# Channel-major products as 512 streamed columns over 256-column weight groups, with x scaled ahead of the products

## The chip, the cores and the metric

The kernel runs on one core of a Trainium2 chip. The metric is the device time of one execution in microseconds; lower is better. The engines are TensorE (PE, with its weight loads shown as PEld), VectorE (DVE), ScalarE (ACT), GpSimd (POOL) and SyncE (SP, which here only starts transfers). Times of stages and instructions come from one profiled execution.

## What is computed

One residual layer with three token-mixer branches over 256 tokens of width 2048, in float32. x is normalised, multiplied by one wide matrix (18464 columns), split among attention, a state-space branch and memory attention, gated, projected and summed. The part that matters here:

```python
def rms_norm(x, w):
    xf = x.astype(jnp.float32)
    y = xf * lax.rsqrt(jnp.mean(xf * xf, axis=-1, keepdims=True) + NORM_EPS)
    return (y * w.astype(jnp.float32)).astype(x.dtype)
...
    h = rms_norm(x, norm_w[layer])
    proj = h @ w_in[layer]
    (sb_q, sb_k, sb_v, sb_z, ssd_z, ssd_xbc, ssd_dt,
     mem_q, mem_z, gate_pre) = jnp.split(proj, offsets, axis=-1)
...
    mem_n = rms_norm(mem, mem_norm_w[layer])
    kv = mem_n @ w_kv
```

## The kernel before

Float32 products are made of three fast products. Every operand is split into a high part (rounded to the fast format) and a low part (what is left), and a product is high by high, high by low and low by high. `split` makes both parts: ScalarE writes the high part (line 143), VectorE subtracts it from the source (line 147, or line 149 where a scale per partition goes in). The activations are kept channel-major, channels on the partitions: `memT` for mem and `hT` for x, 16 k-tiles of 128 channels by 256 tokens, high and low parts in tiles of their own (`Cols`).

`gemm` (line 204) walks over the 16 k-tiles in chunks of two. For each chunk a 512 KB block of weights is loaded on SP's queue (`load_chunk`, `raw`, four buffers) and split into `wh` and `wl` (three buffers each), then come the matmuls, then `pump()`. There are two forms:

- rows (lines 231 to 236): the activations are the stationary operand, 512 weight columns stream past; result tokens by channels. Per k-tile 6 matmuls of 512 columns.
- columns (lines 220 to 230): 128 weight columns are stationary, 256 tokens stream past; result channel-major. Per k-tile and group of 128 weight columns three matmuls of 256 columns: `wh` with the high part, `wh` with the low part, `wl` with the high part.

Columns are used for the memory keys (1024 weight columns), for memory q, memory z, attention z, q and k (1024 each) and for the 4096 convolution channels; rows for everything else.

The order on every engine is written out by the program: nothing is reordered. `pump()` runs once per chunk. It calls what `defer(fn, n)` put n chunks ahead, and takes one step from one of two `lanes` of generators (even chunks one lane, odd chunks the other). So the work around a product stands at fixed places between its chunks; an engine takes its instructions in that order.

Normalisation before: hT is split from x times `norm_w` without the token's own factor, as soon as x is there (`x_pairs`, from the middle of the second product on). The sums of squares are made channel-major from the same x tiles: ScalarE squares 1024 elements at a time (line 296), GpSimd adds the four tiles (lines 297 to 300), TensorE sums over partitions (line 306). `scale_steps` makes 1/rms per token, as a column (`rs_x`) and spread over all partitions (`rbc_x`). That factor is applied at the end of each product that reads hT: on VectorE by a multiply with `rbc_x` (lines 247, 256, 631) for columns, as a scale per partition for rows (lines 272, 615, 770).

The start of the program is: values of the memory (two row products, 10 and 8 chunks), memory keys (two column products of 8 chunks), then memory q from hT.

Of the kernel before, what the change touches and what calls it, by code (L numbers as in the profile page):

```python
# [16 lines left out]
P = 128  # L17
# [4 lines left out]
KC = 2  # L22
EPS = 1e-6
# [3 lines left out]
XLAG = 8  # L27
# [13 lines left out]
def trunk_kernel(  # L41
    ctx: ExitStack,
    tc: tile.TileContext,
    x, x_cols, mem_cols, w_cols, w_in, b_gate, dt_bias, a_log,
# [11 lines left out]
    psA = ctx.enter_context(tc.tile_pool(name="psA", bufs=4, space=bass.MemoryType.PSUM))  # L56
# [94 lines left out]
    class Cols:  # L151


        def __init__(self, nk, n):
            self.hi = [slot([P, 8, T], F32R, n + "h") for _ in range(nk // 8)]
            self.lo = [slot([P, 8, T], F32R, n + "l") for _ in range(nk // 8)]

        def at(self, kt):
            return self.hi[kt // 8][:, kt % 8], self.lo[kt // 8][:, kt % 8]
# [44 lines left out]
    def gemm(lhs, nk, w, c0, evac, cols=False, along=None, sizes=None):  # L204


        acc = [psA.tile([P, GW], F32, tag="acc", name=nm("acc")) for _ in range(2)]
        k0 = 0
        for kc in sizes or [KC] * (nk // KC):
# [6 lines left out]
            for j in range(kc):  # L216
# [3 lines left out]
                if cols:  # L220
                    for b in range(4):
                        a = acc[b // 2][:, (b % 2) * T:(b % 2 + 1) * T]
                        bs = slice(b * P, (b + 1) * P)
                        nc.tensor.matmul(a, wh[:, j, bs], lh, start=first and b % 2 == 0,  # L224
                                         stop=False, skip_group_check=True)
                        nc.tensor.matmul(a, wh[:, j, bs], ll, start=False, stop=False,  # L226
                                         skip_group_check=True)
                        nc.tensor.matmul(a, wl[:, j, bs], lh, start=False, stop=last,  # L228
                                         skip_group_check=True)
                    continue  # L230
# [8 lines left out]
        if cols:  # L239
            acc = [a.rearrange("p (b t) -> p b t", t=T) for a in acc]  # L240
        defer(lambda: evac(acc))

    def to_cols(dst, b0, scale):

        def evac(acc):
            for pr in range(2):
                nc.vector.tensor_tensor(dst[:, b0 + 2 * pr:b0 + 2 * pr + 2], acc[pr],
                                        scale.unsqueeze(1).to_broadcast([P, 2, T]), ALU.mult)
        return evac

    def to_split_cols(dst, b0, scale):
        def evac(acc):
            parts = []
            for pr in range(2):
                u = tmp.tile([P, 2, T], F32, tag="cu", name=nm("u"), bufs=2)
                nc.vector.tensor_tensor(u, acc[pr], scale.unsqueeze(1).to_broadcast([P, 2, T]),
                                        ALU.mult)
                bs = slice(b0 + 2 * pr, b0 + 2 * pr + 2)
                parts.append((dst.hi[0][:, bs], dst.lo[0][:, bs], u, None))
            defer(lambda: split(*parts), 1)  # L260
        return evac
# [7 lines left out]
    def to_rows(dst, c0, scales):  # L269
        def evac(acc):  # L270
            for t in range(2):
                nc.scalar.activation(dst[:, t, c0:c0 + GW], acc[t], AF.Copy,
                                     scale=scales[:, t:t + 1])
        return evac
# [13 lines left out]
    def squares(raw, acc, q, first=None):  # L288

        sq = t4([P, 4, T], "sq")  # L290
        a = 0
        if first is not None:
            nc.scalar.activation(sq[:, 0], first, AF.Square)
            a = 1
        k = 4 * (q % 2)
        nc.scalar.activation(sq[:, a:4], raw[q // 2][:, k + a:k + 4], AF.Square)
        nc.gpsimd.tensor_tensor(sq[:, 0:2], sq[:, 0:2], sq[:, 2:4], ALU.add)
        if q:
            nc.gpsimd.tensor_tensor(sq[:, 0], sq[:, 0], sq[:, 1], ALU.add)
# [624 lines left out]
```

## Time and profile before

| | us |
|---|---|
| median of 3 executions | 1248.94 (1248.73 to 1250.66) |
| the profiled execution, own time | 1249.63 |
| its span | 1247.6 |
| TensorE busy | 1234.8 |
| VectorE busy | 775.9 |
| ScalarE busy | 596.3 |
| GpSimd busy | 123.2 |

The granted TensorE clock is 0.999 of full speed over the span. The stages by the first matmul of each form: row products from 5.7 us, column products from 54.5, rows from 351.4, columns (the convolution channels) from 487.3, rows from 681.5 to the end; single products of the branches run between the chunks.

A matmul's record is longer than its turn: consecutive records overlap. How long one matmul holds TensorE is read from the distance between the starts of two, not from its duration.

### The profile page before, as it was taken

What the parts mean: (1) busy time and instruction counts of PE and PEld (TensorE: products, weight loads), DVE (VectorE), ACT (ScalarE), POOL (GpSimd) and SP (SyncE); (2) the same over time, 40 slices, a digit from 0 to 9 for tenths busy, and PEclk for the clock granted to TensorE, in tenths of its full rate; (3) what the DMA queues carried; (4) which work ended last, traced back from release to release, by engine and by line L of the source; (5) the groups of instructions that cost most, each with busy time, mean ns of one, the idle gap of its engine ahead of it and who ended that gap; (6) DMA issues with size and microseconds to landing.
All of it is one profiled execution on the core that took longest, in us unless ns stands there. A gap on an engine that the chain in (4) does not pass through costs nothing.

```text
span 1247.6 us, 18787 instructions
## 1 busy us (share of the span) xinstructions
PE 1234.8 (99%) x7512; PEld 1108.9 (89%) x7512; DVE 775.9 (62%) x997; ACT 596.3 (48%) x734; POOL 123.2 (10%) x130
## 2 busy tenths in 40 slices
PE   8999999999999999999999999999999999999997
PEld 6899999999988888999999888888888888888886
DVE  7674564555544555688888876676766555555554
ACT  6643443453434545444654545555554444444443
POOL 3510000000000000010100202022211110110101
PEclk9999999999999999999999999999999999999999
DMA  8666565655566656555656656666555666567573
GB/s 295 216 209 174 164 189 174 183 158 164 153 187 197 185 174 183 169 172 169 171 174 196 217 169 220 177 223 199 190 165 182 207 198 196 189 193 245 199 238 123
DMA packets 124680, 236.57 MB, mean 190 GB/s; under 512 B 10128, under 2 KB 11568, under 8 KB 124464
## 3 DMA queue, kind: packets, MB, share of 16 engines
q1 hardware_dynamic: 118272, 224.01, 58.2%
q10 hardware_dynamic: 6320, 11.35, 2.6%
q8 instruction: 59, 0.97, 0.3%
q14 instruction: 29, 0.24, 0.1%
HBM read 233.20 MB, written 2.13 MB: 189 GB/s over the span
## 4 chain that ended last, share of the span: by engine, by line
PE 94%; DMA 2%; ACT 1%; DVE 1%; issue 1%; POOL 0%; SPq 0%; POOLq 0%; ACTq 0%; DVEq 0%
PE acc L234 17%; PE acc L236 17%; PE acc L235 17%; PE acc L224 12%; PE acc L228 12%; PE acc L226 12%; DMA raw<-in_w_mem_kv_dram 2%; PE y L709 1%; DVE wl L147 1%; PE acc L881 1%; PE acc L879 1%; PE acc L880 1%; ACT wh L143 0%; PE off L711 0%; PE dtp L401 0%
## 5 line engine op out<-in xcount | busy, mean ns | idle before, releaser
L147 DVE TENSOR_TENSOR wl<-raw,wh 128x1024 fp32r<-128x1024 f32 (+1 forms) x410 | 510.1, 1245 | 365.6 <-ACT wh L143 364.2
L143 ACT ACTIVATE wh<-raw 128x1024 fp32r<-128x1024 f32 (+1 forms) x410 | 431.9, 1054 | 523.5 <-PE acc L236 265.5
L224 PE MATMUL acc<-hTh,wh 128*128 128x256 f32 x1152 | 327.4, 284 | 0.0
L226 PE MATMUL acc<-hTl,wh 128*128 128x256 f32 x1152 | 325.9, 283 | 0.0
L228 PE MATMUL acc<-hTh,wl 128*128 128x256 f32 x1152 | 325.9, 283 | 0.0
L234 PE MATMUL acc<-wh,hTh 128*128 128x512 f32 x576 | 227.7, 395 | 0.0
L236 PE MATMUL acc<-wh,hTl 128*128 128x512 f32 x576 | 224.5, 390 | 0.0
L235 PE MATMUL acc<-wl,hTh 128*128 128x512 f32 x576 | 224.3, 389 | 0.0
L226 PEld LDWEIGHTS acc<-hTl,wh 128*128 128x128 f32 x1152 | 221.1, 192 | 0.0
L224 PEld LDWEIGHTS acc<-hTh,wh 128*128 128x128 f32 x1152 | 221.0, 192 | 0.1
L228 PEld LDWEIGHTS acc<-hTh,wl 128*128 128x128 f32 x1152 | 221.0, 192 | 0.0
L236 PEld LDWEIGHTS acc<-wh,hTl 128*128 128x128 f32 x576 | 108.1, 188 | 22.9
L235 PEld LDWEIGHTS acc<-wl,hTh 128*128 128x128 f32 x576 | 108.3, 188 | 21.7
L234 PEld LDWEIGHTS acc<-wh,hTh 128*128 128x128 f32 x576 | 108.2, 188 | 21.6
L783 POOL TENSOR_TENSOR merged<-merged,sig 128x512 f32<-128x512 f32 x16 | 27.5, 1744 | 260.2 <-DVE sig L782 222.7
L571 POOL TENSOR_TENSOR lm<-lm,sp 128x384 f32<-128x384 f32 x8 | 11.5, 1435 | 402.3 <-DVE sp L570 402.3
L234 PE MATMUL acc<-wh,oDh 128*128 128x512 f32 x128 | 49.8, 389 | 0.0
L235 PE MATMUL acc<-wl,oDh 128*128 128x512 f32 x128 | 49.8, 389 | 0.0
L236 PE MATMUL acc<-wh,oDl 128*128 128x512 f32 x128 | 49.8, 389 | 0.0
L636 DVE SCALAR_TENSOR_TENSOR cT<-cu,wcols,cT 128x255 f32<-128x255 f32 (+2 forms) x96 | 46.4, 483 | 3.4
L234 PE MATMUL acc<-wh,mTh 128*128 128x512 f32 x96 | 37.4, 390 | 0.0
L236 PE MATMUL acc<-wh,mTl 128*128 128x512 f32 x96 | 37.4, 389 | 0.0
(256 smaller groups left out, 1463.8 us busy)
## 6 DMA issues: line engine op xcount, KB each, us to landing
raw<-in_w_in_dram SPq DMA_DIRECT2D x288, 512.0 KB, 3.8
raw<-in_w_branch_ssd_dram SPq DMA_DIRECT2D x32, 512.0 KB, 4.0
raw<-in_w_out_dram SPq DMA_DIRECT2D x32, 512.0 KB, 4.7
raw<-in_w_mem_kv_dram SPq DMA_DIRECT2D x30, 512.0 KB, 4.9
raw<-in_w_branch_mem_dram SPq DMA_DIRECT2D x16, 512.0 KB, 4.4
raw<-in_w_branch_sb_dram SPq DMA_DIRECT2D x16, 512.0 KB, 4.0
dec<-acT ACTq DMA_DIRECT2D x16, 256.0 KB, 5.7
sig<-in_b_gate_dram ACTq DMA_DIRECT2D x12, 256.0 KB, 4.0
```

The source lines that it names most:

```text
L143: nc.scalar.activation(hi, src, AF.Copy, **({} if scale is None else {"scale": scale}))
L147: nc.vector.tensor_tensor(lo, src, h32, ALU.subtract)
L224: nc.tensor.matmul(a, wh[:, j, bs], lh, start=first and b % 2 == 0, stop=False, skip_group_check=True)
L226: nc.tensor.matmul(a, wh[:, j, bs], ll, start=False, stop=False, skip_group_check=True)
L228: nc.tensor.matmul(a, wl[:, j, bs], lh, start=False, stop=last, skip_group_check=True)
L234: nc.tensor.matmul(a, lh[:, tt], wh[:, j], start=first, stop=False)
L235: nc.tensor.matmul(a, lh[:, tt], wl[:, j], start=False, stop=False)
L236: nc.tensor.matmul(a, ll[:, tt], wh[:, j], start=False, stop=last)
L636: nc.vector.scalar_tensor_tensor(a[:, s:T], u[:, 0:T - s], convw[:, 3 - s, i:i + 1], a[:, s:T], ALU.mult, ALU.add)
L709: nc.tensor.matmul(y[:, q, xc], dec[e // 2][:, e % 2, q], xs[:, q, xc], start=True, stop=True)
L783: nc.gpsimd.tensor_tensor(merged[t][:, cs], merged[t][:, cs], sig[:, t], ALU.add)
L879: nc.tensor.matmul(acc, lh[:, tt], wh, start=(kt == 0), stop=False)
```

## The change

1. `gemm_cols` takes the place of the column form of `gemm`. It makes 256 weight columns at a time, in chunks of four k-tiles (again 512 KB, now 128 partitions by four rows of 256 columns, 1 KB each). High and low parts of the activations now lie side by side in one tile (`Cols.both`), so one matmul streams 512 columns, high and low, past one `wh` group; `wl` streams the 256 columns of the high part and is added to the second half of the accumulator.
2. The accumulator has two halves, which `fold` adds at the end: ScalarE copies one half out of PSUM, VectorE adds the other. The end is deferred by two chunks (`LATE_C`), in `gemm` by three as before.
3. Sums of squares come from rows: x and mem are loaded again, token-major, in four pieces of 512 KB each, on ScalarE's queue (`load_rows`), and ScalarE squares 512 elements with a running sum (`squares`, two per piece). GpSimd's adds and TensorE's sums over partitions are gone.
4. x is multiplied by `rbc_x` on VectorE before the split (`scale_pair`, line 392), so hT holds the normalised x, and no product's end multiplies by `rbc_x` or `rs_x` any more. x's channel-major load moves from the second product to the key products; its eight `scale_pair` calls stand behind chunk 5 of the keys to chunk 1 of memory q.

The core of the diff:

```diff
+    def gemm_cols(lhs, nk, w, c0, evac, ready=None):
+        acc = psA.tile([P, 2, 2, T], F32, tag="acc", name=nm("acc"), bufs=2)
+        for k0 in range(0, nk, KCC):
...
+            raw = load_chunk(w, c0, 2 * P, k0, KCC)
...
+            for kt in range(k0, k0 + KCC):
+                first, last = kt == 0, kt == nk - 1
+                for b in range(2):
+                    nc.tensor.matmul(acc[:, b], wh[:, kt - k0, b * P:(b + 1) * P],
+                                     lhs.both(kt), start=first, stop=False,
+                                     skip_group_check=True)
+                for b in range(2):
+                    nc.tensor.matmul(acc[:, b, 1], wl[:, kt - k0, b * P:(b + 1) * P],
+                                     lhs.at(kt)[0], start=False, stop=last,
+                                     skip_group_check=True)
+            pump()
+        defer(lambda: evac(acc), LATE_C)
+    def fold(dst, acc):
+        nc.scalar.activation(dst, acc[:, :, 1], AF.Copy)
+        nc.vector.tensor_tensor(dst, acc[:, :, 0], dst, ALU.add)
...
-        nc.scalar.activation(sq[:, a:4], raw[q // 2][:, k + a:k + 4], AF.Square)
-        nc.gpsimd.tensor_tensor(sq[:, 0:2], sq[:, 0:2], sq[:, 2:4], ALU.add)
...
+    def squares(r, ss, q):
+        for t in range(2):
+            nc.scalar.activation(r[t], r[t], AF.Square, accum_out=ss[:, t, q:q + 1])
...
+    def row_squares(src, ss, q):
+        r = load_rows(src, q)
+        defer(lambda: squares(r, ss, q), 3)
...
     def along1(k0):
-        if k0 % 4 == 0:
-            xload(k0, k0 + 4)
...
+        if k0 == 0:
+            row_squares(mem, ss_m, 3)
+        elif k0 < 10:
+            row_squares(x, ss_x, k0 // 2 - 1)
+        elif k0 == 10:
+            defer(lambda: scale_x(scale_steps(rs_x, rbc_x, ss_x)), 3)
+            for k in range(0, NKT, 4):
+                defer(lambda k=k: xload(k, k + 4), 1 + k // 2)
...
+    def scale_pair(k):
+        part = xraw[k // 8][:, k % 8:k % 8 + 2]
+        nc.vector.tensor_tensor(part, part, rbc_x.unsqueeze(1).to_broadcast([P, 2, T]),
+                                ALU.mult)
+        split_cols(xraw, hT, normw, k)
+        x_ready.append(k)
...
     def conv_evac(i0):
         def evac(acc):
...
+            u = tmp.tile([P, 2, T], F32, tag="cu", name=nm("cu"), bufs=2)
+            fold(u, acc)
```

How it moves instructions, at three places. First TensorE where the first key product begins, before. `acc_535` and `acc_536` are accumulators, `memTh` and `memTl` the high and low parts of mem, `wh` and `wl` those of the weights; the last figures are partitions by streamed columns.

```order
L236 MATMUL acc_58_354<-wh_87_506,memTl_5_119 128x512
L224 MATMUL acc_91_535<-memTh_2_116,wh_94_539 128x256
L226 MATMUL acc_91_535<-memTl_4_118,wh_94_539 128x256
L228 MATMUL acc_91_535<-memTh_2_116,wl_95_540 128x256
L224 MATMUL acc_91_535<-memTh_2_116,wh_94_539 128x256
```

One k-tile and 256 weight columns were six matmuls of 256 columns. The same place after the change; `memT` holds both parts, and x2 means twice in a row, once for each group of 128 weight columns.

```order
L259 MATMUL acc_58_347<-wh_103_518,memT_5_119 128x512
L332 MATMUL rbc_107_539<-dg_98_489,ones_81 128x256
L223 MATMUL acc_109_541<-memT_2_116,wh_111_544 128x512 x2
L227 MATMUL acc_109_541<-memT_2_116,wl_112_545 128x256 x2
L223 MATMUL acc_109_541<-memT_2_116,wh_111_544 128x512 x2
```

They are two matmuls of 512 columns and two of 256. Second, ScalarE in the second product (values of the memory), before: `wh` are its chunks' splits, `sq` squares, `hTh` the high part of x.

```order
L143 ACTIVATE wh_63_376<-raw_62_374 128x1024
L143 ACTIVATE wh_66_394<-raw_65_392 128x1024
L296 ACTIVATE sq_68_411<-mraw_11_125 128x1024
L143 ACTIVATE wh_72_418<-raw_71_416 128x1024
L143 ACTIVATE wh_75_436<-raw_74_434 128x1024
L143 ACTIVATE wh_79_458<-raw_78_456 128x1024
L143 ACTIVATE hTh_6_120<-xraw_12_126,wcols_80 128x256 x2
L296 ACTIVATE sq_81_478<-xraw_12_126 128x1024
```

After, in the same product: `rows` are the token-major pieces, a DMA row is the start of a load on ScalarE's own queue, and `ss_m` and `ss_x` collect the sums.

```order
L144 ACTIVATE wh_66_374<-raw_65_372 128x1024
L313 DMA rows_68_378<-in_x_dram 128x2x512
L318 ACTIVATE rows_55_331,ss_m_128<-rows_55_331 128x512 x2
L144 ACTIVATE wh_71_396<-raw_70_394 128x1024
L310 DMA rows_73_400<-in_x_dram 128x512
L310 DMA rows_74_401<-in_x_dram 128x512
L318 ACTIVATE rows_62_354,ss_m_128<-rows_62_354 128x512
L318 ACTIVATE rows_63_355,ss_m_128<-rows_63_355 128x512
```

Between two chunks' splits there now stand one or two load starts and two squares, which wait for a load started two chunks earlier. Third, VectorE in the key products, before (`kTl` is the low part of the keys, `u` a product's end, `hTl` the low part of x):

```order
L147 TENSOR_TENSOR wl_135_887<-raw_133_884,wh_134_886 128x1024
L256 TENSOR_TENSOR u_136_914<-acc_91_535,rbc_m_111 128x512
L256 TENSOR_TENSOR u_137_916<-acc_92_536,rbc_m_111 128x512
L149 SCALAR_TENSOR_TENSOR hTl_9_123<-xraw_13_127,wcols_80,hTh_7_121 128x256 x2
L147 TENSOR_TENSOR wl_141_925<-raw_139_922,wh_140_924 128x1024
L147 TENSOR_TENSOR kTl_17_131<-u_136_914,kTh_16_130 128x512
```

And after, in the second of the four key products:

```order
L148 TENSOR_TENSOR wl_158_779<-raw_156_776,wh_157_778 128x1024
L392 TENSOR_TENSOR xraw_12_126<-xraw_12_126,rbc_x_112 128x512
L150 SCALAR_TENSOR_TENSOR hT_7_121<-xraw_12_126,wcols_80,hT_7_121 128x256 x2
L236 TENSOR_TENSOR u_159_803<-acc_136_643,u_159_803 128x512
L275 TENSOR_TENSOR u_159_803<-u_159_803,rbc_m_111 128x512
L148 TENSOR_TENSOR wl_163_810<-raw_161_807,wh_162_809 128x1024
```

The multiply of x and the fold's add are new in the row of work; all eight pairs of x now stand here.

## Rows read from the trace of the kernel before

**Rows 1.** Windows: length, busy (x instructions) by engine, clock, DMA share, GB/s.

```profile
15.00:20.00 5.00, 5.00 (x24) 3.96 (x23) 4.23 (x6) 5.00 (x11) 2.90 (x2) 1.00 1.05 387
...
200.00:300.00 100.00, 100.00 (x836) 100.00 (x836) 50.98 (x56) 43.82 (x50) 0.00 (x0) 1.00 0.58 171
...
500.00:600.00 100.00, 100.00 (x823) 99.56 (x822) 79.19 (x126) 44.48 (x54) 5.55 (x3) 1.00 0.57 169
```

**Rows 2.** Timeline of PE, a column product: start, us, engine, line, operation, idle before.

```profile
200.28 0.28 PE L224 MATMUL acc<-hTh,wh 128*128 128x256 f32 x1
...
202.67 0.28 PE L228 MATMUL acc<-hTh,wl 128*128 128x256 f32 x1
```

**Rows 3.** Timeline of PE, a row product, two starts twelve matmuls apart.

```profile
33.58 0.39 PE L234 MATMUL acc<-wh,memTh 128*128 128x512 f32 x1
...
36.30 0.39 PE L234 MATMUL acc<-wh,memTh 128*128 128x512 f32 x1
```

**Rows 4.** Timeline of PE where 384 and 256 columns alternate, four matmuls.

```profile
490.16 0.34 PE L580 MATMUL scu<-sph,ra 128*128 128x384 f32 x1
490.34 0.28 PE L582 MATMUL scu<-sph,rb 128*128 128x256 f32 x1
...
490.74 0.28 PE L224 MATMUL acc<-hTh,wh 128*128 128x256 f32 x1
```

**Rows 5.** Groups by form: line, engine, operation, count | busy, mean ns | idle before, releaser.

```profile
L147 DVE TENSOR_TENSOR wl<-raw,wh 128x1024 fp32r<-128x1024 f32 x406 | 507.3, 1251 | 359.8 <-ACT wh L143 358.4
L143 ACT ACTIVATE wh<-raw 128x1024 fp32r<-128x1024 f32 x406 | 429.3, 1058 | 520.6 <-PE acc L236 265.5 <-PE acc L226 178.3 <-issue 44.5
...
L780 DVE TENSOR_TENSOR merged<-acc,sig 128x512 f32<-128x512 f32 x8 | 5.1, 681 | 0.0
L615 ACT ACTIVATE zD<-acc,rs_x 128x512 f32<-128x512 f32 x8 | 5.0, 676 | 0.0
...
L812 ACT ACTIVATE junk<-yo 128x512 f32<-128x512 f32 x6 | 3.8, 627 | 6.7 <-DVE yo L810 6.7
...
L721 ACT ACTIVATION_READ_ACCUMULATOR xs<-xn 128x1 f32 x16 | 3.0, 187 | 0.0
```

**Rows 6.** Waits of ACT, 560 to 650 us: us in total, times, longest us.

```profile
ACT wh L143 <- PE acc L226: 27.0, 17, 2.5
```

**Rows 7.** Timeline of PE, places in the first 62 us where its starts stand apart.

```profile
28.27 0.40 PE L234 MATMUL acc<-wh,memTh 128*128 128x512 f32 x1
...
29.77 0.53 PE L236 MATMUL acc<-wh,memTl 128*128 128x512 f32 x1 [0.37 <-DVE memTl L149]
...
45.83 0.50 PE L306 MATMUL ss<-ones,sq_m 128*128 128x1 f32 x4
46.19 0.49 PE L234 MATMUL acc<-wh,memTh 128*128 128x512 f32 x1
...
61.02 0.39 PE L228 MATMUL acc<-memTh,wl 128*128 128x256 f32 x1 [0.38 <-DVE wl L147]
```

**Rows 8.** Timelines of DVE, POOL and ACT: splits beside GpSimd's adds and alone, a load's start.

```profile
27.09 1.75 DVE L147 TENSOR_TENSOR wl<-raw,wh 128x1024 fp32r<-128x1024 f32 x1
...
27.84 1.59 POOL L300 TENSOR_TENSOR sq_m<-sq,sq_m 128x256 f32<-128x256 f32 x1
...
86.00 1.22 DVE L147 TENSOR_TENSOR wl<-raw,wh 128x1024 fp32r<-128x1024 f32 x1 [0.26 <-ACT wh L143]
87.14 0.87 DVE L149 SCALAR_TENSOR_TENSOR hTl<-xraw,wcols,hTh 128x256 fp32r<-128x256 f32 x2
...
0.78 0.41 ACTq L371 DMA_DIRECT2D head<-in_mem_cols_dram  x1
```

**Rows 9.** DMA issues, 20 to 45 us: queue, count, KB each, median us to landing.

```profile
xraw<-in_x_cols_dram SPq DMA_DIRECT2D x3, 512.0 KB, 8.1
```

**Rows 10.** DMA queue of the weights, whole span: packets, MB, share of 16 engines.

```profile
q1 hardware_dynamic: 118272, 224.01, 58.2%
```

**Rows 11.** DMA queue of the ACT writes, 1234 to 1247.6 us.

```profile
q10 hardware_dynamic: 576, 0.66, 13.9%
```

More of the change, by code (lines that the diff above doesn't have):

```diff
@@ L22 @@
 KC = 2
+KCC = 4
 EPS = 1e-6
@@ L154, in __init__, with at, both @@
         def __init__(self, nk, n):
[L155 to L159, printed above, removed]
+            self.hl = [slot([P, 4, 2, T], F32R, n) for _ in range(nk // 4)]
+        def at(self, kt, n=None):
+            s = self.hl[kt // 4]
+            k = kt % 4 if n is None else slice(kt % 4, kt % 4 + n)
+            return s[:, k, 0], s[:, k, 1]
+        def both(self, kt):
+            return self.hl[kt // 4][:, kt % 4]
     lanes = [deque(), deque()]
@@ L219, in gemm @@
                 first, last = kt == 0, kt == nk - 1
[L220 to L230, printed above, removed]
                 for t in range(2):
@@ L286, in split_cols, with load_rows, scale_steps @@
         split(*[(*dst.at(k), raw[k // 8][:, k % 8], w[:, k:k + 1]) for k in (k0, k0 + 1)])
[L288 to L295, printed above, removed]
-        nc.scalar.activation(sq[:, a:4], raw[q // 2][:, k + a:k + 4], AF.Square)
-        nc.gpsimd.tensor_tensor(sq[:, 0:2], sq[:, 0:2], sq[:, 2:4], ALU.add)
-        if q:
-            nc.gpsimd.tensor_tensor(sq[:, 0], sq[:, 0], sq[:, 1], ALU.add)
-        nc.gpsimd.tensor_tensor(acc, sq[:, 0], acc if q else sq[:, 1], ALU.add)
-    def scale_steps(rs, rbc, acc):
-        ps = bank([P, 2], "ss")
+    def load_rows(src, q):
+        cs = slice(q * GW, (q + 1) * GW)
+        if q % 2:
+            r = [ta([P, GW], "rows") for _ in range(2)]
+            for t in range(2):
+                nc.scalar.dma_start(r[t], src[t * P:(t + 1) * P, cs])
+            return r
+        r = t4([P, 2, GW], "rows")
+        nc.scalar.dma_start(r, src[:, cs].rearrange("(t p) n -> p t n", p=P))
+        return [r[:, t] for t in range(2)]
+    def squares(r, ss, q):
         for t in range(2):
-            nc.tensor.matmul(ps[:, t:t + 1], acc[:, t * P:(t + 1) * P], ones[:, 0:1],
-                             start=True, stop=True)
-        yield
+            nc.scalar.activation(r[t], r[t], AF.Square, accum_out=ss[:, t, q:q + 1])
+    def scale_steps(rs, rbc, ss):
         ms = small([P, 2], "ms")
-        nc.vector.tensor_scalar(ms, ps, 1.0 / D, EPS, ALU.mult, ALU.add)
+        nc.vector.tensor_reduce(ms, ss, AX.X, ALU.add)
+        nc.vector.tensor_scalar(ms, ms, 1.0 / D, EPS, ALU.mult, ALU.add)
         nc.gpsimd.tensor_tensor(rs, ms, mhalf, ALU.pow)
```

129 lines of the change are left out of this document (61 added, 68 removed).

## The prediction

> **What bounds the kernel now.** I read the windows first. From 200 to 300 us TensorE is busy all the time, in a stretch of column products, while VectorE is busy half of it and ScalarE less [rows 1]. In the convolution stage, the fullest for VectorE, TensorE is still busy all the time and VectorE 79.19 of 100 us [rows 1]. ScalarE's splits are mostly held back by TensorE: of 520.6 us idle before `wh`, 265.5 and 178.3 end with a matmul [rows 5]; in the convolution stage it waited 17 times in 90 us [rows 6]. So the other engines run ahead until the three weight buffers are full, and from about 62 us to the tail the time is the number of matmuls times the turn of each.
>
> The turn is the distance between starts. Twenty column matmuls of 256 streamed columns take 2.39 us [rows 2], 119.5 ns each; twelve row matmuls of 512 take 2.72 us [rows 3], 226.7 ns each. The clock is the full 2.4 GHz (1.00 in [rows 1]), at which 256 columns alone are 106.7 ns and 512 are 213.3. So each matmul costs its columns and about 13 ns on top, whatever its width. That a mixture keeps this law is seen where 384 and 256 columns alternate: four matmuls from 490.16 to 490.74 [rows 4], 0.58 us for 1280 columns (533 ns) and four times 12 ns.
>
> Only the start is different. Between 5 and 62 us there are places where TensorE's starts stand apart [rows 7], because VectorE is late, and transfers run at 387 GB/s with all 16 DMA engines busy [rows 1].
>
> **The change part by part.**
>
> *Fewer, wider matmuls.* Per k-tile and 256 weight columns, six turns of 119.5 ns become two of 226.7 and two of 119.5: 717.0 against 692.4 ns, 24.6 ns less. By the 13.3 ns on top of a 512-column turn it is two such amounts, 26.6. The column products have 40 groups of 256 weight columns (4 for the keys, 20 for the five blocks of 1024, 16 for the convolution), times 16 k-tiles, 640 in all: 15.7 to 17.0 us, taken as 16.3. All of it is on the path, since TensorE has no gap there. A chunk of a column product goes from 24 × 119.5 = 2.87 us to 8 × 226.7 + 8 × 119.5 = 2.77 us.
>
> A page speaks against this term: the Trainium skill, "TensorE: Matmul & The Clock Gate", section "Back-to-back issue gap", gives a gap of N/2.4 plus 2.5 ns, so a matmul saved would be worth 2.5 ns and not 13. Rows 2 and 3 differ from it, and the measured turn decides; what it would give is among the rivals.
>
> *The ends of products.* Per 512 weight columns VectorE had two multiplies out of PSUM and now has two adds, both about 0.68 us (nearest row, `merged` [rows 5]): nothing. In the convolution four multiplies of 256 elements become two adds of 512: a little less. ScalarE gets two copies of 512 elements out of PSUM, 0.68 us each (`zD` [rows 5]), 27 us over the 40 products; with `wh` at 1.06 it is then busy some 1.2 of each 2.77 us. Cover: it is up to three weight tiles ahead. What is new is a coupling: VectorE's add waits for ScalarE's copy, the copy for the product's last matmul, and behind them stand the next `wh` and `wl`. The end comes two chunks (5.5 us) after the last matmul's chunk in program order, and copy, `wh` and `wl` take 0.68 + 1.06 + 1.25 = 3.0 us. It holds with 2.5 us to spare. Bounds: 0, and 4 us (0.1 us at each of 40 ends, since a miss costs the excess alone); nearer to 0: taken 0.5.
>
> *GpSimd's adds and TensorE's partition sums go.* A `wl` split beside a GpSimd add takes 1.75 us, alone 1.22 [rows 8]. The two matmuls from 28.27 to 29.77 [rows 7] took 1.50 instead of 0.45 us, waiting for VectorE in such a stretch: 1.05 us. The sum over partitions holds TensorE from 45.83 to 46.19 [rows 7], 0.36 us, and once more for x: 0.7. The wait at 61.02 [rows 7] costs about 0.5. Together −2.3 us.
>
> *Row pieces in the first two products.* Eight loads of 512 KB (4.2 MB) join from the eighth chunk on, while x's channel-major 2.1 MB move to the keys, where there is room. Over about 25 us the demand is nine weight chunks (4.7 MB) and the rows, 8.9 MB or 356 GB/s against the 387 seen [rows 1]: near full. A 512 KB load in the crowded stretch landed after 8.1 us [rows 9]; the squares come about two chunks (5.4 us) after the start, so ScalarE can stand up to 2.7 us. Its work per chunk is `wh` 1.06, two squares of 0.63 with a read of the sum of 0.19 each [rows 5], 1.63, and one or two load starts of 0.41 [rows 8]: 3.1 to 3.5 us against TensorE's 2.72 for twelve row matmuls. Over seven chunks that is 2.7 to 5.6 us of lead used up, with the 2.7 at most 8.3. Against it stands a lead of two chunks and the squares that go earlier in the first product. Bounds 0 and 8 us. I take 1.5, near the lower end, because ScalarE is normally ahead [rows 5].
>
> *x scaled in the key products.* For each of eight pairs VectorE does the multiply (0.68), waits for ScalarE's first half (0.5), does two low parts (0.87 [rows 8]), waits about 0.5 for `wh`, then `wl` (1.22): 3.8 us where a chunk lasts 2.77. Eight pairs, five chunks with `wl` alone, and three ends of keys with a fold, a multiply and a low part (2.0) make 42.5 us in 13 chunks, which last 36.0. The excess of 6.5 us meets a lead of two to three chunks (5.5 to 8). Bounds 0 and 4 us, taken 1.5.
>
> *DMA shape.* The weights of column products come in rows of 1 KB. The whole weight queue used 58.2% of 16 engines' 1247.6 us for 118272 packets, nearly all of 2 KB [rows 10]: 98 ns each. The writes at the end, 1.15 KB a packet on average, took 13.9% of 16 × 13.6 us for 576 [rows 11]: 52.5 ns. By that a chunk's 512 packets need 512 × 52.5/16 = 1.68 us of 2.77: hidden, cost nothing. What if not is the last rival.
>
> *Sum,* on the profiled execution (1249.6 of its own, span 1247.6): 1249.6 − 16.3 − 2.3 + 0.5 + 1.5 + 1.5 = 1234.5. The median shown is 0.7 lower, so 1233.8, rounded to 1233.5.
>
> **The rivals.**
>
> - *The start is dear.* The row loads and the scaling cost their upper bounds, 8 and 4 us instead of 3 together: 1242.5. For it: the 8.1 us landing and the 356 of 387 GB/s. Against it: four `raw` buffers and ScalarE's lead.
> - *A matmul saved is worth little.* If the 13 ns came with streamed columns and not with each matmul, and only 2.5 ns went with each, the gain is 640 × 2 × 2.5 ns = 3.2 us: 1246.5. Rows 2 to 4 speak against it. It is the page's rule named above.
> - *The column stages stop following TensorE.* VectorE and ScalarE wait for each other so long that the chunk stays at 2.87 us: the gain is lost, and the start's 1.2 us are added: about 1250. For it: VectorE is at 79% in the convolution. Against it: ScalarE's waits for TensorE there [rows 6].
> - *The 1 KB rows make the weight transfers the bound: slower.* It decides from 86.6 ns a packet on (16 × 2.77 us/512). If a 1 KB packet took as long as a 2 KB one, 98 ns, a chunk would need 3.14 us, and the 160 chunks of column products 160 × (3.14 − 2.87) = 43 us more than before: 1249.6 + 43 + 1.2 − 0.7 = 1293. Rows 11 speak against it, though they are writes.
>
> **How the numbers follow.** The forecast, 1228 to 1239, has 0.72; the dear start 0.13; the small saving 0.03; the lost gain 0.05; the slow transfers 0.07. The low end of the range, 1228, is the sum with 17.0 us and the three open terms at 0 to 0.5 (1249.6 − 0.7 − 17.0 − 2.3 − 1 for what GpSimd's absence may give beyond the two places). The high end, 1242, reaches to the dear start and leaves out the last three. A measurement of this kernel tells about 0.2% from no change, 2.5 us. Faster by more: 0.72 + 0.13 = 0.85; within: 0.03 + 0.05 = 0.08; slower: 0.07.
>
> **What would show it.** After the change 16 column matmuls should take 2.77 us, with no idle time of TensorE between 100 us and the tail; a window of 100 us in the column stages should hold some 578 matmuls. `wl` in the first 60 us should take 1.2 us, not 1.75. The weight queue's share in the column stages should stay under 0.75. The places to look for new waits are ScalarE's squares between 25 and 50 us (released by a load of `rows`) and VectorE's splits between 65 and 100 us. I am wrong if the turn in the alternation is not 226.7 and 119.5, if TensorE waits for `wl` or `wh` in the column stages, or if the start loses more than 8 us.

## The result, and the profile of the changed kernel

The changed kernel takes 1236.8 us (1235.77 to 1237.86), the kernel before, run beside it, 1249.07 us (1248.73 to 1250.66). The ratio is 0.9899, with a 95% interval of 0.9882 to 0.9916: 12.3 us or 1.0% faster. Forecast were 1233.5 us, in a range of 1228 to 1242.

The profiled execution of the changed kernel took 1237.6 us, with a span of 1235.9; before, these were 1249.63 and 1247.6. The two spans differ by 11.7 us. The first matmuls of each stage show where that lies:

| from the first matmul of ... to the next stage's | before, us | after, us | change |
|---|---|---|---|
| start, row products of mem | 48.77 | 49.14 | +0.4 |
| column products up to the first row product of the middle | 296.89 | 288.77 | -8.1 |
| row products of the middle | 135.91 | 135.91 | 0 |
| convolution, column products | 194.26 | 188.51 | -5.75 |
| last row products, to the last matmul | 557.55 | 559.08 | +1.5 |
| after the last matmul | | | +0.24 |

So 13.9 us were won where column products run, and about 2 us lost elsewhere. The windows of after, the changed kernel (length, busy time and count by engine, granted clock, DMA share, GB/s), answer to [rows 1]:

```profile
100.00:200.00 100.00, 100.00 (x590) 87.71 (x589) 58.76 (x84) 46.45 (x57) 0.46 (x1) 1.00 0.65 185
200.00:300.00 100.00, 100.00 (x594) 88.08 (x594) 54.74 (x59) 49.61 (x60) 0.00 (x0) 1.00 0.59 176
500.00:600.00 100.00, 100.00 (x579) 87.65 (x579) 85.46 (x136) 52.41 (x67) 7.39 (x4) 1.00 0.59 178
```

TensorE is still busy all the time in the column stages, now with 594 matmuls in a window that held 836 [rows 1]; VectorE in the convolution rose from 79.19 to 85.46 of 100 us and still follows. The DMA share stays at 0.59 to 0.65.

The timeline of TensorE in a column product of after (start and length in us; equal neighbours are drawn together) answers to [rows 2]:

```profile
250.22 0.63 PE L223 MATMUL acc<-hT,wh 128*128 128x512 f32 x2
250.69 0.39 PE L227 MATMUL acc<-hT,wl 128*128 128x256 f32 x2
250.92 0.62 PE L223 MATMUL acc<-hT,wh 128*128 128x512 f32 x2
251.38 0.40 PE L227 MATMUL acc<-hT,wl 128*128 128x256 f32 x2
...
252.31 0.40 PE L223 MATMUL acc<-hT,wh 128*128 128x512 f32 x1
```

From 250.22 to 252.31 lie three k-tiles: 697 ns for two matmuls of 512 and two of 256 columns. The sum had 692.4. The starts of this kernel between 200 and 340 us put the wide matmuls 233 ns and the narrow ones 115 to 116 ns apart, where the sum had 226.7 and 119.5: in this mixture the wide turn is dearer and the narrow one cheaper than in a stream of equals.

The groups of after that answer to [rows 5], and the weight queue that answers to [rows 10]:

```profile
L148 DVE TENSOR_TENSOR wl<-raw,wh 128x1024 fp32r<-128x1024 f32 x406 | 502.7, 1241 | 329.5 <-ACT wh L144 327.1
L318 ACT ACTIVATE rows<-rows 128x512 f32<-128x512 f32 x16 | 9.9, 622 | 5.5 <-DMA rows<-in_mem_dram 2.1 <-DMA xraw<-in_x_cols_dram 1.8 <-DMA raw<-in_w_mem_kv_dram 1.4
L235 ACT ACTIVATE cu<-acc 128x512 f32<-128x512 f32 x16 | 9.6, 598 | 27.6 <-PE acc L227 27.6
L144 ACT ACTIVATE hT<-xraw,wcols 128x256 fp32r<-128x256 f32 x16 | 7.3, 502 | 17.6 <-DVE xraw L392 17.6
...
q1 hardware_dynamic: 159232, 224.01, 58.7%
```

The squares of the row pieces waited 5.5 us for loads in all. The copies at the ends of convolution products (`cu`) wait 27.6 us for TensorE's last matmul, and TensorE waits for nothing there. ScalarE stands 17.6 us for the scaling of x. And the weight queue took the same bytes in 40960 more packets in the same share of time.

Two places were not in the forecast. In the key products TensorE waits for low weights, and near the end for VectorE (waits, then timeline of TensorE with the idle time before a matmul and its releaser):

```profile
PE acc L227 <- DVE wl L148: 1.1, 2, 0.5
...
1214.36 0.40 PE L912 MATMUL acc<-wlh,mT 128*128 128x512 f32 x1
1215.66 0.38 PE L910 MATMUL acc<-wlh,mT 128*128 128x256 f32 x1 [0.90 <-DVE yo L840]
```

The last start stands 1.30 us behind the one before, where a turn is 0.23 (and where the kernel before took 0.23 at the same place). TensorE wants an accumulator that the output block before the last still holds, and VectorE (timeline) has not yet read its second half:

```profile
1213.19 0.68 DVE L840 TENSOR_TENSOR yo<-acc,xr 128x512 f32<-128x512 f32 x1
1214.67 0.15 DVE L846 TENSOR_REDUCE fs<-ssy 128x1 f32<-128x3 f32 x1 [0.79 <-ACT junk L842]
1214.86 0.15 DVE L847 TENSOR_SCALAR msy<-fs 128x1 f32<-128x1 f32 x1
1214.93 0.68 DVE L840 TENSOR_TENSOR yo<-acc,xr 128x512 f32<-128x512 f32 x1
```

Between the two additions VectorE waits 0.79 us for ScalarE and does two small instructions. Before, the accumulators were four tiles of 512 float32 a partition; now they are two of 1024, and the last product's second accumulator has to wait until both halves of that block are read.

### The profile page after: what moved, and what is told of

Same layout as the page of the kernel before. It is cut to its first block, busy times and chain, and to the rows that moved or that the text cites. A ratio compares the mean times of both kernels' runs of the same rounds, so it can differ in the third digit from the quotient of the medians.

```text
span 1235.9 us, 16263 instructions
## 1 busy us (share of the span) xinstructions
PE 1221.2 (99%) x6224; PEld 1037.7 (84%) x6224; DVE 769.2 (62%) x995; ACT 616.6 (50%) x797; POOL 93.8 (8%) x108
## 3 DMA queue, kind: packets, MB, share of 16 engines
q1 hardware_dynamic: 159232, 224.01, 58.7%
## 4 chain that ended last, share of the span: by engine, by line
PE 93%; DMA 4%; DVE 1%; ACT 1%; issue 0%; SPq 0%; ACTq 0%; POOLq 0%; POOL 0%; DVEq 0%
PE acc L223 23%; PE acc L258 17%; PE acc L259 17%; PE acc L257 17%; PE acc L227 12%; PE y L741 1%; DMA raw<-in_w_mem_kv_dram 1%; DMA mraw<-in_mem_cols_dram 1%; DMA raw<-in_w_out_dram 1%; DVE wl L148 1%; DMA xraw<-in_x_cols_dram 1%; ACT wh L144 0%; PE acc L910 0%; PE off L743 0%; PE acc L912 0%; PE acc L911 0%
## 5 line engine op out<-in xcount | busy, mean ns | idle before, releaser
L223 PE MATMUL acc<-hT,wh 128*128 128x512 f32 x1152 | 363.2, 397 | 0.0
L227 PEld LDWEIGHTS acc<-hT,wl 128*128 128x128 f32 x1152 | 216.4, 188 | 51.2
L257 PE MATMUL acc<-wh,hT 128*128 128x512 f32 x576 | 227.8, 396 | 0.0
L227 PE MATMUL acc<-hT,wl 128*128 128x256 f32 x1152 | 226.6, 278 | 0.0
L259 PE MATMUL acc<-wh,hT 128*128 128x512 f32 x576 | 224.5, 390 | 0.0
L258 PE MATMUL acc<-wl,hT 128*128 128x512 f32 x576 | 224.4, 390 | 0.0
L223 PEld LDWEIGHTS acc<-hT,wh 128*128 128x128 f32 x1152 | 175.5, 189 | 0.1
L259 PEld LDWEIGHTS acc<-wh,hT 128*128 128x128 f32 x576 | 108.1, 188 | 23.0
L258 PEld LDWEIGHTS acc<-wl,hT 128*128 128x128 f32 x576 | 108.3, 188 | 21.8
L257 PEld LDWEIGHTS acc<-wh,hT 128*128 128x128 f32 x576 | 108.2, 188 | 21.6
L257 PE MATMUL acc<-wh,oD 128*128 128x512 f32 x128 | 49.8, 389 | 0.0
L259 PE MATMUL acc<-wh,oD 128*128 128x512 f32 x128 | 49.8, 389 | 0.0
L813 POOL TENSOR_TENSOR merged<-merged,sig 128x512 f32<-128x512 f32 x16 | 27.6, 1743 | 260.3 <-DVE sig L812 233.5
L257 PE MATMUL acc<-wh,mT 128*128 128x512 f32 x96 | 37.4, 390 | 0.0
L259 PE MATMUL acc<-wh,mT 128*128 128x512 f32 x96 | 37.4, 389 | 0.0
```

The lines of the kernel that those rows point to most:

```text
L223: nc.tensor.matmul(acc[:, b], wh[:, kt - k0, b * P:(b + 1) * P], lhs.both(kt), start=first, stop=False, skip_group_check=True)
L227: nc.tensor.matmul(acc[:, b, 1], wl[:, kt - k0, b * P:(b + 1) * P], lhs.at(kt)[0], start=False, stop=last, skip_group_check=True)
L257: nc.tensor.matmul(a, lh[:, tt], wh[:, j], start=first, stop=False)
L258: nc.tensor.matmul(a, lh[:, tt], wl[:, j], start=False, stop=False)
L259: nc.tensor.matmul(a, ll[:, tt], wh[:, j], start=False, stop=last)
L813: nc.gpsimd.tensor_tensor(merged[t][:, cs], merged[t][:, cs], sig[:, t], ALU.add)
```

## The experiments

Every kernel below is the changed kernel with one edit (the last but one has two, the last none). Its median stands beside 1236.8 us, and 1237.39 us where the changed kernel was run again on the same chip. The kernel before gave 1249.1 to 1249.3 beside all of them. The diffs are shortened: `..` stands for arguments left out, and some loop bodies are told in words.

### What a matmul saved is worth: six narrow ones again

```diff
-                for b in range(2):
-                    nc.tensor.matmul(acc[:, b], wh[.., b], lhs.both(kt), ..)
-                for b in range(2):
-                    nc.tensor.matmul(acc[:, b, 1], wl[.., b], hi, ..)
+                for b in range(2):
+                    nc.tensor.matmul(acc[:, b, 0], wh[.., b], hi, ..)
+                    nc.tensor.matmul(acc[:, b, 1], wh[.., b], lo, ..)
+                    nc.tensor.matmul(acc[:, b, 1], wl[.., b], hi, ..)
```

> The column products issue three 256-column matmuls per block and k-tile again (six for a pair of blocks), on the weight groups, tiles, row sums and scaling of the changed kernel. Theory (fixed part per matmul): 640 pairs of k-tile and group go back from 697 ns to 6 x 119.8 = 718 to 719 ns, +13.5 to +14.5 us against the changed kernel, so 1250 to 1251.5 us, as slow as the kernel before. Rival (a matmul saved is worth 2.5 ns, the rest of the gain came from something else): 1280 matmuls more at 2.5 ns, +3.2 us, about 1240. Second rival (the gain was the column stages' freedom from the adds on GpSimd, not the matmuls): +0, about 1237.

Measured: 1249.98 us (1247.72 to 1251.31); its ratio to the kernel before is 1.0004 (0.9995 to 1.0013). The whole gain is gone with this one edit, so the matmuls are the gain; the rest of the change, with its row sums, its scaling and its end, comes out at +0.9 us. In every kernel here each matmul has a weight load of its own (7504 of both in this one, 6224 in after), so what is shown is the worth of a matmul together with its weight load; no run tells the two apart. Timeline of TensorE, two starts 24 matmuls apart:

```profile
250.09 0.28 PE L225 MATMUL acc<-hT,wh 128*128 128x256 f32 x1
...
252.97 0.28 PE L225 MATMUL acc<-hT,wh 128*128 128x256 f32 x1
```

2.88 us for 24 is 120.0 ns a turn, 720 a k-tile. Of 577 groups of three matmuls between 100 and 340 us that stand between others of their kind, 573 take 360 ns exactly. Against 696.8 ns (the mean of 279 k-tiles of after in the same stretch) the change saves 23.2 ns a k-tile, 14.8 us over 640. Two matmuls are saved, 11.6 ns each. The gap of 2.5 ns on top of the columns, which the Trainium skill, "TensorE: Matmul & The Clock Gate", section "Back-to-back issue gap", gives for a single matmul by itself, would have left this run near 1240; the trace, a stream of matmuls each with its weight load, differs from it.

### Why 697 and not 692: orders and lengths

The first edit lets a 256 follow each 512:

```diff
                 for b in range(2):
                     nc.tensor.matmul(acc[:, b], wh[.., b], lhs.both(kt), ..)
-                for b in range(2):
                     nc.tensor.matmul(acc[:, b, 1], wl[.., b], hi, ..)
```

> The same four matmuls per k-tile, in the order 512, 256, 512, 256 columns rather than 512, 512, 256, 256. Theory (each 512-column matmul followed by another of a new block costs 233 ns rather than 227, and the one after it is no cheaper): a turn of 691 to 693 ns rather than 697, -2.5 to -3.5 us, about 1234. Rival (the moving operand of both parts costs the same wherever it stands): turn 697 ns, within 0.5 us of the changed kernel. Third way (a short matmul behind a long one hides less of the next weight load): turn 700 to 710, +2 to +8 us.

Measured: 1242.81 us (1242.23 to 1243.81), 6 us slower than the changed kernel. Timeline of TensorE, two starts 16 matmuls (four k-tiles) apart:

```profile
250.14 0.40 PE L224 MATMUL acc<-hT,wh 128*128 128x512 f32 x1
...
252.97 0.40 PE L224 MATMUL acc<-hT,wh 128*128 128x512 f32 x1
```

That is 707 ns a k-tile (706 in the mean of the stage). In size it was the third way named ahead; the reason given there, the weight load, is not shown. I then took the number of changes of length for the cause, and made two kernels: one with half as many changes, and one with none, where the low weights stream 512 columns too.

```diff
-            for kt in range(k0, k0 + KCC):
-                2 x 512 (wh); 2 x 256 (wl)
+            for k2 in range(k0, k0 + KCC, 2):
+                4 x 512 (wh of k2, k2 + 1); 4 x 256 (wl of k2, k2 + 1)
```

> The column products take two k-tiles at a time: four matmuls of 512 columns, then four of 256. Theory (what costs is the change of length: a turn of equal matmuls has 13.3 ns over its columns each, the pair of changes in the turn of 697 ns 3.7 ns, and the order 512, 256, 512, 256 with four changes took 706.6 ns): one pair of changes per two k-tiles, 695 ns a turn, -1.2 us against the changed kernel, 1235.6. Rival (the moving operand of both parts costs 233 ns wherever it stands): 697 ns, within 0.4 us.

```diff
                 for b in range(2):
-                    nc.tensor.matmul(acc[:, b, 1], wl[.., b], lhs.at(kt)[0], ..)
+                    nc.tensor.matmul(acc[:, b], wl[.., b], lhs.both(kt), ..)
```

> The low weights stream both parts too (the product of low by low is added): four 512-column matmuls per k-tile. Theory (change of length costs): 4 x 226.7 = 907 ns a turn against 697, 640 x 210 = +134 us, about 1371. Rival (the moving operand of both parts costs 233 ns): 932 ns, +150 us, about 1387. Rival on the transfers (the column products' 1 KB rows are close under their limit): neither helps to tell, since the products get slower.

Timelines of TensorE, first of the kernel with four and four (two starts, two k-tiles apart), then of the one with 512 columns only (two starts, three k-tiles apart):

```profile
250.31 1.09 PE L223 MATMUL acc<-hT,wh 128*128 128x512 f32 x4
...
251.71 1.09 PE L223 MATMUL acc<-hT,wh 128*128 128x512 f32 x4
```

```profile
250.16 0.62 PE L223 MATMUL acc<-hT,wh 128*128 128x512 f32 x2
...
252.88 0.39 PE L223 MATMUL acc<-hT,wh 128*128 128x512 f32 x1
```

The second took 1370.25 us (a single execution) and 907 ns a k-tile, 226.7 a matmul: streaming both parts of `hT` costs nothing over the row products' 226.7 [rows 3], and that rival falls. But the first took 1238.45 us (1237.85 to 1239.25) and 701 ns a k-tile: half the changes of length, and 4 ns more, not 2 less. So my count of changes falls too. A last kernel mirrored the blocks of the two short matmuls, so that neighbours write the same block `b` of the accumulator, which the expectation calls a bank:

```diff
-                for b in range(2):
+                for b in (1, 0):
                     nc.tensor.matmul(acc[:, b, 1], wl[.., b], lhs.at(kt)[0], ..)
```

> The two matmuls of 256 columns in the other order of blocks (second block, then first), so that the second 512 and the first 256 add to the same bank, and so do the second 256 and the next 512. Theory A (banks: two matmuls in a row on one bank are what made the order 512, 256, 512, 256 dearer): a turn of about 705 ns rather than 697, +5 us. Theory B (lengths alone): 697, within 0.4 us. Theory C (alternation of banks is what costs 3.5 ns here): 693, -2.2 us.

Measured: 1237.17 us (1236.95 to 1237.94) and 696.8 ns, the same. Which block the neighbours write is not it. What is shown: equal matmuls follow each other at their columns and 13.3 ns, with almost no scatter, 256 as well as 512; mixed ones cost 3.5 (512, 512, 256, 256), 7.7 (four and four) or 12.6 ns (512, 256, 512, 256) more per k-tile, by the order. Why stays open. The order of the changed kernel is the cheapest of the three.

### The wait in the key products

```diff
         nc.vector.tensor_tensor(part, part, rbc_x.., ALU.mult)
+        defer(lambda: split_pair(k), 1)
+
+    def split_pair(k):
         split_cols(xraw, hT, normw, k)
```

> The product of a pair of x chunks by the row scale is issued on VectorE one step ahead of the pair's split instead of right before it. Theory: the hand-over between VectorE and ScalarE in the key products no longer stands once per pair in the path, the three waits for wl at 92 to 99 us (0.79, 0.36 and 0.80 us) go, -1.5 to -2.0 us: 1235. Rival: VectorE is full there (the pairs are bounded by its sum of work, not by the hand-over): waits of the same sum, within 0.4 us.

Measured: 1235.41 us (1234.29 to 1236.18), 1.4 below the changed kernel, and no wait of TensorE between 55 us and the last product. The windows of 55 to 100 us, first of after, then of this kernel:

```profile
55.00:100.00 45.00, 43.85 (x249) 37.46 (x248) 35.87 (x50) 25.17 (x37) 0.00 (x0) 1.00 0.62 191
```

```profile
55.00:100.00 45.00, 45.00 (x260) 39.27 (x259) 36.79 (x51) 26.07 (x40) 0.00 (x0) 1.00 0.71 207
```

The stage of the first column products lasts 286.80 us rather than 288.77, -1.97 us. VectorE's work is the same; what stood in the path is the hand-over, which the timeline of VectorE in after shows for one pair:

```profile
63.91 0.68 DVE L392 TENSOR_TENSOR xraw<-xraw,rbc_x 128x512 f32<-128x512 f32 x1
65.17 0.89 DVE L150 SCALAR_TENSOR_TENSOR hT<-xraw,wcols,hT 128x256 fp32r<-128x256 f32 x2 [0.58 <-ACT hT L144]
66.52 1.23 DVE L148 TENSOR_TENSOR wl<-raw,wh 128x1024 fp32r<-128x1024 f32 x1 [0.47 <-ACT wh L144]
67.67 0.68 DVE L392 TENSOR_TENSOR xraw<-xraw,rbc_x 128x512 f32<-128x512 f32 x1
```

That is 3.76 us a pair, of which 1.05 are waits for ScalarE. In all VectorE waits 6.2 us for ScalarE in this window of after; the lead covers most of it, and 2.0 reach TensorE.

### The wait ahead of the last product

The first try put two of the three accumulators on one tile:

```diff
+    ends = [psA.tile([P, 2, GW], F32, tag="acc", bufs=2)]
     for t in range(2):
         for cs in ..:
-            acc = psA.tile([P, 2, GW], F32, tag="acc", bufs=2)[:, 0, ..]
+            if cs.start:
+                ends.append(psA.tile([P, 2, GW], F32, tag="acc", bufs=2))
+            acc = ends[-1][:, t if not cs.start else 0, ..]
```

> In the last product the first two accumulators share one two-bank tile, and the third takes the other tile, so that it need not wait for the block before last to be added on VectorE. Theory: the gap of 1.30 us ahead of its first matmul near 1215.7 us falls to a turn of about 0.23, -1.07 us: 1235.7. Rival: the matmuls reach the end sooner but the last additions and the output transfer are what end the span: 0 to -0.3 us.

Measured: 1241.62 us (1237.87 to 1242.52), slower by 4.8. I had taken the waiting matmul for that of the third accumulator; it is the second one's. On a shared tile it waits for VectorE's reading of the first accumulator, which itself comes late and ends at 1218.19. Timelines of VectorE and TensorE, and the window behind the wait:

```profile
1217.77 0.42 DVE L852 TENSOR_TENSOR yo<-acc,xr 128x256 f32<-128x256 f32 x1
...
1214.41 0.39 PE L914 MATMUL acc<-wlh,mT 128*128 128x512 f32 x1
1218.24 0.56 PE L912 MATMUL acc<-wlh,mT 128*128 128x256 f32 x1 [3.44 <-DVE yo L852]
...
1219.03 0.41 PE L912 MATMUL acc<-wlh,mT 128*128 128x256 f32 x1
1219.24 0.41 PE L913 MATMUL acc<-wll,mT 128*128 128x256 f32 x1
...
1218.00:1222.00 4.00, 3.76 (x19) 3.76 (x20) 1.82 (x5) 1.64 (x4) 0.98 (x2) 0.57 0.14 56
```

The wait took 3.83 us from start to start, and in the four microseconds behind it the granted clock is 0.57, its lower level of 1.2 GHz for most of them: turns of 213 ns for 256 columns, where 120 is the rule. Sixteen such turns cost another 1.5 us. With the 3.6 us of the wait that is 5.1, of which after had 1.07 already: the 4.0 us by which this span is longer than that of after.

The second try leaves the tiles and puts both additions first:

```diff
         def evac(acc):
             for t in range(2):
-                out_half(t, g, acc[t], xr[:, t])
+                nc.vector.tensor_tensor(yo[t][:, cs], acc[t], xr[:, t], ALU.add)
+            for t in range(2):
+                out_half(t, g, None, None)
```

(`out_half` skips its own addition when it is handed none, and does the squares and the mean alone.)

> In the output product's blocks both additions of x come before the first half's squares and mean, so that the accumulator is free after two additions (1.3 us) rather than after an addition, a wait of 0.79 us for ScalarE, two small instructions and an addition (2.4 us). Theory: the gap of 1.30 us ahead of the last product's second accumulator falls to about 0.25 us, -1.0 us: 1235.8. Rival (what ends the span is the chain of the last additions and transfers, started by VectorE): 0 to -0.3 us.

Measured: 1236.0 us (1235.32 to 1237.3), -0.8 with ranges that overlap, and no wait of TensorE near the end. How much the old order costs hangs on when VectorE has split the last weights: of the ten profiles with the old order and tiles the gap is 0.63 to 1.31 us in nine, and a plain turn of 0.23 in one, the kernel with 512 columns only. In this kernel's profile the weights came early (the additions began at 1211.77, 1.4 us earlier than in after), so there even the old order would have been in time. The kernel below that has this edit too shows it where time is short, in the timelines of VectorE and of TensorE:

```profile
1211.44 1.28 DVE L889 TENSOR_TENSOR yo<-acc,xr 128x512 f32<-128x512 f32 x2
...
1212.84 0.32 PE L917 MATMUL acc<-wlh,mT 128*128 128x256 f32 x1
```

The additions end at 1212.72, 0.12 us before the accumulator is written again. In the old order the second one ends 2.42 us after the first begins (1213.19 to 1215.61 in after), here at 1213.86, a wait of a microsecond.

### The start

Two edits belong here. One fills an idle stretch of TensorE, because in the profile of after the granted clock is low right behind it (two windows of after, then the second of before):

```profile
10.00:14.00 4.00, 2.42 (x10) 1.46 (x8) 1.42 (x2) 1.86 (x3) 0.00 (x0) 1.00 0.99 296
14.00:18.00 4.00, 4.00 (x10) 3.01 (x11) 2.61 (x5) 2.43 (x4) 0.00 (x0) 0.57 0.99 364
...
14.00:18.00 4.00, 4.00 (x17) 3.17 (x18) 3.22 (x6) 4.00 (x8) 1.37 (x2) 1.00 1.06 389
```

Ten matmuls of 512 columns in the second window, where the profile of before has 17 at 1.00: about 1.6 us lost.

```diff
             split_cols(mraw, memT, memw, k0)
+            if k0 == 4:
+                keep_warm(16)
```

> Sixteen small matmuls on a tile of ones (67 ns each) stand on TensorE's queue where it waits for the fifth block of mem near 11.4 us, so its idle stretch of 1.4 us is cut to under 0.5. Theory (the stretch without matmuls near 11.4 us is what the granted clock falls after, in some executions): no window at 0.57 to 0.71 between 14 and 18 us, and no run near 1237.6, median 1235.9. Rival (the clock's fall comes with the whole uneven start, as at 6 us in another run): the fall moves or stays, median 1236.8.

Measured: 1236.81 us (1235.86 to 1238.47), the same. Its windows:

```profile
6.00:10.00 4.00, 4.00 (x10) 3.22 (x11) 3.11 (x7) 2.85 (x6) 0.00 (x0) 1.00 0.89 281
...
14.00:18.00 4.00, 4.00 (x32) 3.79 (x32) 3.08 (x7) 2.99 (x5) 0.00 (x0) 1.00 1.04 395
```

The slow turns (427 ns) are now between 6 and 10 us, behind the other idle stretch of TensorE from 4.4 to 5.9; the column of the clock shows 1.00 there, the ten matmuls in 4 us do not. The median is what the rival said, but this run settles little, for two reasons. The slow turns stand at that earlier place in five profiles without this edit too, so nothing shows that the filling moved them. And the filling was longer than meant: the sixteen matmuls stand in the profile as 32, which hold TensorE from 13.27 to 16.76 us, 3.5 us where the expectation's 67 ns make 1.1.

Of the 13 profiles of the changed kernel and its variants, eleven have six to eleven slow matmuls, five of them behind the stretch at 11 us and six behind the one at 4 us, never both; two have none, nor has the profile of before, though idle stretches of the same length stand in all three. So what decides between a fall and none stays open. Among those with the same start code, the start lasts 49.1 us in the mean of nine with slow matmuls and 47.9 in the two without: 1.2 us.

The other edit takes the row pieces away:

```diff
     def row_squares(src, ss, q):
-        r = load_rows(src, q)
-        defer(lambda: squares(r, ss, q), 3)
+        if q == 0:
+            nc.vector.memset(ss, 512.0)
```

> The rows of mem and x are not loaded and their sums of squares not taken: the sums are a constant, so this kernel leaves out the scales by row. Theory (the row pieces cost the start: 8 transfers of 0.5 MB on queues that are full to 55 us, and squares on ScalarE ahead of splits): the waits for the low weights near 45 and 52 us (0.84 and 0.37 us gaps) go, the first column product starts 1 to 3 us earlier than 54.9 us, and x is there earlier; 1234 to 1235.5. Rival (the row pieces cost nothing, what bounds the start is the weights and mem alone): within 0.4 us of the changed kernel.

Measured: 1236.2 us (1235.79 to 1236.7), 1.2 below the changed kernel on the same chip. Windows of 18 to 55 us, first of after, then without the rows:

```profile
18.00:55.00 37.00, 36.55 (x161) 29.64 (x159) 22.09 (x32) 28.25 (x57) 2.54 (x3) 1.00 1.02 367
```

```profile
18.00:55.00 37.00, 37.00 (x165) 30.61 (x164) 23.14 (x35) 20.13 (x25) 1.62 (x3) 1.00 0.83 286
```

Without them TensorE does not wait at all there, the DMA engines are no longer full (0.83), and ScalarE does 8 us less. The waits that go (0.45 us of idle time in the first place, near 45 us) are those that the first theory named. The first column product starts at 54.12 us, after a start of 48.49 that has slow matmuls near 15 us; the four others that have them there took 48.2 to 49.1. So 0.1 us by the profiles and 1.2 by the medians: the row pieces cost something between these two, and the scatter of the start (47.7 to 49.6 us with the same code) does not let it be told closer.

### Both waits taken away, and the changed kernel again

> Both the multiplication of x one step ahead and the two additions ahead of the squares. Theory (the two waits stand in the path one after the other and are free of each other): the gains add, -1.9 and -1.0 us against the changed kernel on the same chip, -2.9. Rival (what is won at 100 us is lost again to a later wait): under -2.0.

> The changed kernel itself, beside the others on this chip: 1236.8 us, its runs 1235.8 to 1237.9, with the start (first column product) anywhere from 53.5 to 55.4 us as in the profiles so far.

Measured: 1234.47 us (1233.94 to 1234.71) with the multiply one step ahead and the additions first, 1237.39 us (1236.8 to 1238.1) for the changed kernel itself. The difference is 2.9 us, as was expected, though the two edits alone gave 1.4 and 0.8 by their medians. The stages show it better than the medians: the first column products last 286.80 us against 288.77 and 288.79 in the two profiles of the changed kernel, and the last row products, to the last matmul, 557.89 against 559.08 and 559.50. So the waits do not replace each other. The kernel with both has no wait of TensorE left between 55 us and the end, and is the fastest that was run; its ratio to the kernel before is 0.9879 (0.9862 to 0.9895). The start in the changed kernel's second profile is 47.74 us, within 47.7 to 49.6 of all with that code.

## Why the forecast held, and where its terms were off

**The matmuls.** The mechanism was right: a fixed part per matmul, whatever its width, and no gap to lose it in. The term was -16.3 and is -14.8 us by the turns, -13.2 by the medians with and without it. Two steps of it were off, in opposite directions. The narrow turn is 120.0 ns, not 119.5: twenty matmuls read in hundredths of a microsecond [rows 2] leave half a nanosecond open, which over the four that go is 2 ns a k-tile. And the law was carried over to mixtures from four matmuls in 0.58 us [rows 4], where the last digit is 2.5 ns a matmul; the mixture here costs 3.5 ns a k-tile more than the law. Of the 1.6 us between the turns and the medians 1.1 lie in the key products: beyond its turns (384 k-tiles) the first column stage holds 20.1 us of other work and waits with narrow matmuls, 21.2 in after and 19.2 with the multiply a step ahead, so at 720 ns a k-tile more than half of those waits is hidden.

**The ends of products.** Taken 0.5, measured 0.2 at most: TensorE has no idle time from 100 us to the last product, though ScalarE's copies wait 27.6 us for it, and the convolution won 5.75 us where its 256 k-tiles by 23.2 ns make 5.94. The lead was long enough.

**GpSimd and the partition sums.** -2.3 was right in its mechanism: all early low parts of 1024 weights a partition take 1.22 to 1.23 us, the gaps at 28 and 61 us are gone, and so are the sums over partitions. But only part of it shows in the sum. In the key products about 1.1 us went: 384 k-tiles at -23.2 ns are -8.9, the waits there give back +1.9, and the stage lost 8.1. Of that 1.1, which is what is left of the stage, 0.9 are seen to go: the wait at 61 us (0.54) and the sum over partitions for x (0.36). In the start the rest is hidden by the row pieces and by the slow matmuls.

**Row pieces.** Taken 1.5 within 0 to 8; the run without them puts them between 0.1 and 1.2. The mechanism, ScalarE's order behind late pieces, is there (TensorE waits near 45 and 52 us), but the squares waited only 5.5 us in all, so the lead was nearly enough.

**x scaled in the key products.** Taken 1.5 within 0 to 4; it is 2.0 by the stage and 1.4 by the medians. The pair takes 3.76 us where the sum had 3.8, and all waits come at the end of the lead, at 92 to 99 us.

**Not in the forecast.** The accumulators in two tiles of double size: I costed the ends of products, and not the last product, whose second accumulator now waits 1.07 us for VectorE. That is the step that was left out: a change of buffers from four to two was in the diff, and what is late next there was not asked. The slow matmuls of the start, about 1.2 us in most executions, are a second miss; the profile of before had none, and nothing in it could have told. That the start still came out at +0.4, close to its share of the sum, is luck: dearer row pieces were expected, and slow matmuls came.

Put together from what was measured: 1249.6 - 14.8 (turns) - 1.1 (GpSimd, keys) + 1.9 (scaling) + 0.4 (start, all in all) + 1.1 (tail) = 1237.1, against 1237.6 of the profiled execution. The forecast's 1233.5 was 3.3 us low: 1.5 from the turns, 1.1 from the tail, 0.4 from the scaling, 0.3 from rounding down; the ends of products (-0.5) and the start with GpSimd's part (about +0.1) nearly cancel, and half a microsecond is not placed.

Two of the forecast's own signs of being wrong did come, both small: the turn in the alternation is 697 ns and not 692.4, and TensorE waits for `wl` in the key products, at 92 to 99 us. The third, a start that loses more than 8 us, did not.

**The rivals.** The dear start did not come: 49.14 us against 48.77. The small saving fell with the six narrow matmuls. The column stages did not stop following TensorE, with VectorE at 85%. The slow transfers did not come either: the weight queue's time is the same for the same bytes; if the 77312 packets of 2 KB still take 98 ns, the 81920 of 1 KB took 49 ns each (58.7% of 16 × 1235.9 us, less 77312 × 98 ns, over 81920), where the last output writes had let me expect 52.5 [rows 11].

## What to carry to other kernels

Where TensorE is never idle, count matmuls as well as columns: here each one less, with its weight load, was worth 11.6 ns, but take the turn from a stretch long enough for a tenth of a nanosecond, and measure a mixture of widths before multiplying it by hundreds. When a change makes buffers fewer and larger, go through every user of the pool, the last one too, and ask who reads the buffer's predecessor and what stands ahead of that read on its engine. The waits of a pair of engines that hand work to and fro reach the path once the lead is used up (here 2.0 of 6.2 us); issuing one side a step earlier gave these 2 us back, and putting releases ahead of sums about another.

## What the hardware showed unexpectedly

- Equal matmuls with a new weight tile each keep an exact turn (120.0 ns for 256 columns, 226.7 for 512), and a mixture does not: 697, 701 or 706 ns for the same four matmuls, by their order alone; in the cheapest order the wide ones take 233 ns and the narrow ones 115 to 116. The cause stays open.
- TensorE's granted clock fell behind an idle stretch of 3.6 us near the end (0.57 in the window after it, 213 ns for 256 columns), and behind stretches of 1.1 to 2.2 us at the start in eleven of thirteen profiles, at one of two places; in the one profile with the later stretch filled the fall stood at the earlier. Stretches of 1.3 to 1.7 us in the two others and in before, and the 1.07 us lost ahead of the last product in after, were followed by none.
- The weight queue moved 224.01 MB in 58.2% of the engines' time with 118272 packets and in 58.7% with 159232: no fixed part per packet shows between rows of 2 KB and of 1 KB.
